# Gain rows of a two-layer decoder put on all partitions by a transpose and by way of memory, instead of by matmuls with diagonals

## The chip, the cores and the metric

The kernel runs on one core of a Trainium2 chip. The metric is the device time of one execution in microseconds (us). PE is TensorE, PEld its weight load, DVE is VectorE, ACT is ScalarE, POOL is GpSimd, SP is SyncE.

## The reference

A decoder of two layers with one sequence of 512 tokens, a model width of 1024, all in fp32. A conditioning vector `c` gives six vectors of 1024 per layer (shift, scale and gain for the mixer, the same for the MLP), by a product with a large matrix. The first layer's mixer is a pooling over windows, the second's a gated unit (SGU).

```python
c_act = jax.nn.silu(c)
for i in range(DEPTH):                                   # 2 layers
    mod = c_act @ ada_w[i] + ada_b[i]                    # 6 x 1024
    sh1, sc1, g1, sh2, sc2, g2 = jnp.split(mod, 6, axis=-1)
    h = modulate(rmsnorm(x, norm_mix_g[i]), sh1, sc1)    # h * (1 + sc) + sh
    y = pool_mixer(h, ...) if i == 0 else sgu_mixer(h, ...)
    x = x + g1[:, None, :] * y
    h = modulate(rmsnorm(x, norm_mlp_g[i]), sh2, sc2)
    x = x + g2[:, None, :] * sq_relu_mlp(h, mlp_w1[i], mlp_w2[i])   # square(relu(h @ w1)) @ w2
return rmsnorm(x, final_g)
```

The change is about `g1` and `g2`: a gain has one value per channel, and the tile `x` has tokens on partitions and channels along a row, so the gain is needed as one row of 1024 that stands alike on all 128 partitions.

## The kernel before, in words

Large products are done as three matmuls each (`mm3`, lines 178 to 180): both operands are split into a high and a low part of a reduced type. ScalarE makes the high part (line 169), VectorE the low part by a subtraction (line 170).

Products of the conditioning vector are done on VectorE: `ada_tile` loads 128 columns of the large matrix (512 KB) into a work buffer of tag `w4` (there are three of these, and raw weights take the same three) and sums them against the vector `cb` (line 200). The results are columns: `mods[i]` has 48 columns of 128 values for layer i, and a gain takes eight of them (`c_g`). The columns become a row on all partitions in `spread_cols`: GpSimd multiplies the identity by each of the eight columns (`diagonals`, line 209), which gives eight 128x128 diagonals in one tile `dg`; two matmuls of a matrix of ones against four diagonals each (line 218, in fp32, not split) put the row on all partitions in PSUM; two ScalarE copies (line 219) bring it into `gb`, one tile of 128x1024 that all gains share in turn. `gated` (line 966) and `fold` (line 837) read it.

There are three spreads. The first, the gain of the first MLP, is an entry of the list `ex` that `mlp` works off beside the matmuls: 33 entries, spread over the units of work by a quota `due`. It stands ninth, behind the eight `ada_tile`s that make its columns. The second, the gain of the SGU, is the first entry of the list in the SGU part, called in `do_u(0)`, after the unit's matmuls. The third, the gain of the second MLP, is in `mlp(1)`, where the diagonals are made ahead (tile `dgu`) and the matmuls come after the unit `("f", (0, 7))`. The first gain of the first layer goes another way that the change doesn't touch.

`mlp(i)` is a list of units: "f" a tile of the up projection, "s" and "p" products of a scheme with seven products in place of eight for the up and the down projection, "q" the rest of the down projection. Operands of a unit are prepared some units ahead (`ahead`, `prep`). In the second layer the weight sums that this scheme needs are partly made by transfers that add to what stands in the buffer, and these are issued by GpSimd:

```python
def b_add(t, c, r, n):
    G.dma_start(t, w2[i, c, r, n], accum_op=ALU.add)      # line 767; line 703 is the like for w1
```

Such a weight tile `bt` (1 MB) is split, added to, split again, added to, and so on. TensorE's instructions run in the order of the code. Those of the other engines and of their DMA queues are ordered at compile time by a scheduler from readiness and the order of the code (by hand in the first layer's mixer). On each engine and each queue of an engine the order is then fixed, and an instruction that waits holds up those behind it. `sm` is a pool of small tiles; the pools are padded (`shift`) so that tiles start at multiples of 128 words.

Of the kernel before, what the change touches and what calls it, by code (L numbers as in the profile page):

```python
# [7 lines left out]
F32 = mybir.dt.float32  # L8
F32R = mybir.dt.float32r
AF = mybir.ActivationFunctionType  # L10
ALU = mybir.AluOpType
# [3 lines left out]
P = 128  # L15
D = 1024
S = 512
KD = D // P
# [23 lines left out]
def c_sh(n, k):  # L42
    return 24 * n + 2 * k + 1


def c_g(n, k):
    return 24 * n + 16 + k
# [31 lines left out]
def decoder_kernel(ctx: ExitStack, tc: tile.TileContext, xtok, vecs, rows, fgrow, ada0, adag, ada1, pool_w, w1s, w1, w1f, w1b, w2, w2e, w_v, w_u, w_o, wsT, lnp, bs, out):  # L79
    nc = tc.nc  # L80
    V, A, G, T = nc.vector, nc.scalar, nc.gpsimd, nc.tensor
# [3 lines left out]
    w4 = ctx.enter_context(tc.tile_pool(name="w4", bufs=3))  # L85
    wts = ctx.enter_context(tc.tile_pool(name="wts", bufs=5))
    cp = ctx.enter_context(tc.tile_pool(name="cp", bufs=1))
    sm = ctx.enter_context(tc.tile_pool(name="sm", bufs=3))
# [17 lines left out]
    def bank(name, pool=None):  # L106
        pool = pool or ps
        return pool.tile([P, S], F32, name=name, tag="mm" if pool is ps else "xz")
# [4 lines left out]
    ones = cp.tile([P, P], F32, name="ones")  # L113
# [3 lines left out]
    ident = cp.tile([P, P], F32, name="ident")  # L117
    G.memset(ident, 0.0)
    G.affine_select(out=ident, in_=ident, compare_op=ALU.not_equal, fill=1.0, base=0, pattern=[[-1, P]], channel_multiplier=1)
    mods = [cp.tile([P, 48], F32, name=f"mods{i}") for i in range(2)]  # L120
# [16 lines left out]
    gb = big.tile([P, D], F32, name="gb")  # L137

    def X(t):
        return x_[t // 2][:, t % 2]  # L140

    def H(k, c):

        return h_[0][:, 0, k, c], h_[0][:, 1, k, c]
# [4 lines left out]
    def mod(i, c):  # L149
        return mods[i][:, c : c + 1]  # L150
# [32 lines left out]
    def finish_mods(i, b, pm):  # L183

        V.tensor_tensor(mods[i][:, 2 * b : 2 * b + 2], pm, vec[:, V_ADAB + 48 * i + 2 * b : V_ADAB + 48 * i + 2 * b + 2], ALU.add)
        n, q = divmod(b, 12)
        if q < 8:
            g0 = (V_MIX, V_MLP)[n] + 8 * i + q
            V.scalar_tensor_tensor(scl[i][n][:, q : q + 1], mod(i, 2 * b), 1.0, vec[:, g0 : g0 + 1], ALU.add, ALU.mult)
# [3 lines left out]
    def ada_tile(i, t, src, get):  # L193

        r = get()
        nc.sync.dma_start(r, src)
        b, j = divmod(t, 2)
        if j == 0:
            pmv[i, b] = sm.tile([P, 2], F32, name="pmv", tag="pmv")
        V.scalar_tensor_tensor(r, r, 1.0, cb, ALU.mult, ALU.mult, accum_out=pmv[i, b][:, j : j + 1])  # L200
        if j == 1:
            finish_mods(i, b, pmv.pop((i, b)))
# [1 line left out]
    def get4():  # L204
        return w4.tile([P, D], F32, name="ada", tag="w4")

    def diagonals(dg, cols):
        for k in range(KD):
            G.tensor_scalar(dg[:, k], ident, cols[:, k : k + 1], None, ALU.mult)

    def spread_cols(cols, dg=None):

        if dg is None:
            dg = w4.tile([P, KD, P], F32, name="dg", tag="w4")
            diagonals(dg, cols)
        for n in range(2):
            po = bank("pb")
            T.matmul(po, ones, dg[:, 4 * n : 4 * n + 4], start=True, stop=True)  # L218
            A.activation(gb[:, S * n : S * n + S], po, AF.Copy)


    def power(v, n):
# [12 lines left out]
    with (  # L235
# [67 lines left out]
        def rms():  # L303
            v0 = sm.tile([P, NT], F32, name="rv4", tag="rv4")
            V.tensor_scalar(v0, ss, RMS_EPS, None, ALU.add)
            rt.append(power(v0, NT))
# [217 lines left out]
        def norm_lo(k):  # L524
# [8 lines left out]
            sm=sums_of, rms=rms, edge=edges, bandr=bands, m=m, n=n_, nf=n_fin, fin=fin, gm=gm, gt=gt, gc=gc, bc=bc, we=we,  # L533
# [58 lines left out]
    def parts(o, a):  # L592

        A.activation(o[0], a, AF.Copy)
        V.tensor_tensor(o[1], a, f32(o[0]), ALU.subtract)

    def mlp(i, first, extra, last, ending):
# [3 lines left out]
        with (  # L601
# [56 lines left out]
            def a_sums(step):  # L658


                def a(r, j):
                    return h32[0][:, 4 * j : 4 * j + 4, 256 * r : 256 * r + 256]

                def operand(pool, tag):
                    t = pool.tile([P, 2, 4, 256], F32R, name="as", tag=tag)
                    return t[:, 0], t[:, 1]

                def minus(o, p, q):
                    V.tensor_tensor(o, p, q, ALU.subtract)

                first, half = slice(0, 256), slice(256, 512)
                if step == 0:
                    sums_a.update({1: H(slice(0, 4), first), 2: H(slice(4, 8), first), 4: H(slice(4, 8), half)})
                    shift(hx, LINE - GAP)
                    minus(a(1, 1), a(1, 0), a(1, 1))
                    m, o = 5, operand(hx, "hx")
                elif step == 1:
                    minus(a(1, 1), a(1, 1), a(0, 0))
                    m, o = 6, operand(big, "x0")
                elif step == 2:  # L680
                    minus(a(0, 0), a(0, 0), a(1, 0))
                    V.tensor_tensor(a(1, 1), a(1, 1), a(0, 1), ALU.add)
                    m, o = 3, operand(big, "x1")
                else:
                    m, o = 7, H(slice(0, 4), half)
                parts(o, a(0, 0) if m == 7 else a(1, 1))
                sums_a[m] = o
# [214 lines left out]

            gain = mods[i][:, c_g(1, 0) : c_g(1, 0) + KD]
            done = first(put)
            if i:
                dg = su.tile([P, KD, P], F32, name="dgu", tag="u")
                diagonals(dg, gain)
            units = [("f", (0, f)) for f in range(done, 8)]
            for c in range(3):
                if i == 0:  # L910
# [17 lines left out]
            def ahead(n):  # L928

                if i == 0:  # L930
                    return min(n + 3, len(units))
                m, s = n + 1, items(*units[n])
                while m < len(units) and m < n + 5:
                    s += items(*units[m])
                    if s > 5 and m > n + 1:
                        break
                    m += 1
                return m
# [4 lines left out]
            for n, (kind, u) in enumerate(units):  # L943
                for m in range(n, ahead(n)):
                    if m not in ready:
                        ready[m] = prep[units[m][0]](units[m][1])
                while at < len(extra) and at < due * (n + 1):
                    extra[at]()
                    at += 1
                run[kind](u, ready[n])  # L950
                if i and kind == "f":
                    a_sums(u[1] - 4)
                    if u == (0, 7):
                        spread_cols(gain, dg)
                if i and u == (3, 1, 4):
                    reload()

# [24 lines left out]
    def normed(hf, i, n):  # L982

        xs = []
        for r in range(2):
            t = w4.tile([P, D], F32, name="xs", tag="w4")
            A.activation(t, X(2 * hf + r), AF.Copy, scale=rms(2 * hf + r))
            xs.append(t)
        c = slice(256 * hf, 256 * hf + 256)
        for k in range(0, KD, 2):  # L990
            px = bank("px")
            for q in range(2):
                for r in range(2):
                    T.transpose(px[:, 256 * q + P * r : 256 * q + P * r + P], xs[r][:, P * (k + q) : P * (k + q) + P], ident)  # L994
            tt = h32[0][:, k : k + 2, c] if h32 else sm.tile([P, 2, 256], F32, name="tt", tag="tmp")
            for q in range(2):
                a, b = scl[i][n][:, k + q : k + q + 1], mod(i, c_sh(n, k + q))
                if q:
                    A.activation(tt[:, q], px[:, 256:512], AF.Identity, bias=b, scale=a)
                else:  # L1000
                    V.tensor_scalar(tt[:, q], px[:, 0:256], a, b, ALU.mult, ALU.add)
            parts(H(slice(k, k + 2), c), tt)


    h32, xd = [], []
    dram = ctx.enter_context(tc.tile_pool(name="dram", bufs=1, space=bass.MemoryType.DRAM))

    def spill(h):
        xd.append(dram.tile([P, 2, D], F32, name=f"xd{h}"))
# [2 lines left out]
    def reload():  # L1012
        for h in range(2):
            x_[h] = big.tile([P, 2, D], F32, name=f"x{h}", tag=f"x{h}")
            G.dma_start(x_[h], xd[h])
        load_fg()
# [4 lines left out]
        return SWEEP  # L1021

    ex = [lambda q=q: ada_tile(0, 40 + q, ada1[q], get4) for q in range(8)]
    ex += [lambda: spread_cols(mods[0][:, c_g(1, 0) : c_g(1, 0) + KD])]
    ex += [lambda q=q: ada_tile(1, q, ada1[8 + q], get4) for q in range(24)]
    mlp(0, first0, ex, gated, lambda: normed(0, 1, 0))


# [6 lines left out]
    with (  # L1035
# [27 lines left out]
        for t in range(NT):  # L1063
# [6 lines left out]
            r = rsqrt(ag[:, 1:2], 1.0, LN_EPS, 1)  # L1070
# [2 lines left out]
                V.tensor_tensor(v, v, lnt[:, n].rearrange("p (a b) -> p a b", a=2), op)  # L1073

        u, gt, wu = {}, {}, {}
        ex = [lambda: spread_cols(mods[1][:, c_g(0, 0) : c_g(0, 0) + KD])]
        ex += [lambda q=q: ada_tile(1, q, ada1[8 + q], get4) for q in range(24, 40)]

        def do_u(n):
# [75 lines left out]
    def last1(t, c0, n, src, y):  # L1155
# [13 lines left out]
        else:  # L1169
# [5 lines left out]
            nc.sync.dma_start(out[t, :, 1], X(t)[:, S:D])  # L1175

    mlp(1, first1, [], last1, lambda: None)


# [77 lines left out]
```

## Time and profile before

| | |
|---|---|
| time, median of 3 runs | 872.88 us (872.5 to 873.39) |
| profiled execution | 872.98 us, its span 871.3 us |
| TensorE busy | 858.0 us, 98% of the span |
| VectorE, ScalarE, GpSimd busy | 669.6, 452.0, 66.2 us |
| granted TensorE clock, mean | 0.998 |
| moved by DMA | 161.80 MB, 186 GB/s |
| GpSimd's DMA queue | 4032 packets, 23.07 MB, 13.0% of the engines' time |

Times in the trace are counted from the start of the span. A row of a group gives line, engine, operation, written and read tiles, shapes and count, then the busy time and the mean length of one in ns, then the engine's idle time just before them and what ended most of it. A row of a timeline gives start, length, the instruction, and in brackets the idle time before it with what ended that. The lengths of matmuls are modelled and overlap; the chain in order of time gives each the stretch until the next one.

### The profile page before, as it was taken

What the parts mean: (1) busy time and instruction counts of PE and PEld (TensorE: products, weight loads), DVE (VectorE), ACT (ScalarE), POOL (GpSimd) and SP (SyncE); (2) the same over time, 40 slices, a digit from 0 to 9 for tenths busy, and PEclk for the clock granted to TensorE, in tenths of its full rate; (3) what the DMA queues carried; (4) which work ended last, traced back from release to release, by engine and by line L of the source; (5) the groups of instructions that cost most, each with busy time, mean ns of one, the idle gap of its engine ahead of it and who ended that gap; (6) DMA issues with size and microseconds to landing.
All of it is one profiled execution on the core that took longest, in us unless ns stands there. A gap on an engine that the chain in (4) does not pass through costs nothing.

```text
span 871.3 us, 11810 instructions
## 1 busy us (share of the span) xinstructions
PE 858.0 (98%) x4580; PEld 739.3 (85%) x4580; DVE 669.6 (77%) x884; ACT 452.0 (52%) x656; POOL 66.2 (8%) x87
## 2 busy tenths in 40 slices
PE   8999999999999999999999999999999999999996
PEld 7778888788888888888878888999999998999885
DVE  6889696789869886657798866667777698778755
ACT  5285755554444445238233326666765576566521
POOL 3000002000000000000410012000101000100001
PEclk9999999999999999999999999999999999999999
DMA  9959853553454341615548525937758587667302
GB/s 352 417 224 316 293 179 129 193 193 121 180 206 169 127 163 49 217 33 209 193 159 291 180 73 210 340 78 179 167 196 181 155 230 220 138 160 261 123 24 97
DMA packets 39517, 161.80 MB, mean 186 GB/s; under 512 B 4387, under 2 KB 4515, under 8 KB 34214
## 3 DMA queue, kind: packets, MB, share of 16 engines
q1 hardware_dynamic: 35282, 137.72, 44.1%
q0 software_dynamic: 4032, 23.07, 13.0%
q8 instruction: 36, 0.59, 0.2%
q10 hardware_dynamic: 148, 0.27, 0.1%
q14 instruction: 19, 0.16, 0.0%
HBM read 156.84 MB, written 4.19 MB: 185 GB/s over the span
## 4 chain that ended last, share of the span: by engine, by line
PE 91%; DMA 5%; DVE 1%; ACT 1%; issue 0%; SPq 0%; POOLq 0%; POOL 0%; DVEq 0%; ACTq 0%
PE po L178 17%; PE po L180 17%; PE po L179 17%; PE pm L178 12%; PE pm L179 12%; PE pm L180 12%; DMA wl<-in_ada 2%; DMA wh<-in_ada 1%; DMA raw<-in_w1s 1%; PE po L1099 1%; ACT sq L275 1%; PE px L994 1%; DMA x<-in_xtok 1%; PE pb L218 1%; PE po L566 0%
## 5 line engine op out<-in xcount | busy, mean ns | idle before, releaser
L178 PE MATMUL po<-hb,wl 128*128 128x256 f32 (+1 forms) x624 | 209.7, 336 | 0.4 <-DVE wl L170 0.4
L180 PE MATMUL po<-hb,wh 128*128 128x256 f32 (+1 forms) x624 | 207.8, 333 | 0.0
L179 PE MATMUL po<-hb,wh 128*128 128x256 f32 (+1 forms) x624 | 207.8, 333 | 0.0
L170 DVE TENSOR_TENSOR wl<-raw,wh 128x1024 fp32r<-128x1024 f32 (+1 forms) x110 | 131.1, 1194 | 47.2 <-ACT wh L169 47.1
L169 ACT ACTIVATE wh<-raw 128x1024 fp32r<-128x1024 f32 (+1 forms) x110 | 113.1, 1034 | 64.8 <-PE pm L180 31.9
L179 PE MATMUL pm<-wl,oh 128*128 128x512 f32 x336 | 130.8, 389 | 0.0
L178 PE MATMUL pm<-wh,ol 128*128 128x512 f32 x336 | 130.8, 389 | 0.0
L180 PE MATMUL pm<-wh,oh 128*128 128x512 f32 x336 | 130.8, 389 | 0.0
L178 PEld LDWEIGHTS po<-hb,wl 128*128 128x128 f32 x624 | 117.2, 188 | 14.1 <-DVE wl L170 1.2
L179 PEld LDWEIGHTS po<-hb,wh 128*128 128x128 f32 x624 | 117.2, 188 | 12.9 <-issue 0.5
L180 PEld LDWEIGHTS po<-hb,wh 128*128 128x128 f32 x624 | 118.0, 189 | 11.9
L170 DVE TENSOR_TENSOR wl<-b,wh 128x1024 fp32r<-128x1024 f32 x60 | 72.9, 1223 | 26.6 <-ACT wh L169 26.5
L200 DVE SCALAR_TENSOR_TENSOR ada<-ada,cb 128x1024 f32<-128x1024 f32 x56 | 68.3, 1222 | 15.4 <-DMA ada<-in_ada 15.3
L180 PEld LDWEIGHTS pm<-wh,oh 128*128 128x128 f32 x336 | 63.1, 188 | 13.1
L179 PEld LDWEIGHTS pm<-wl,oh 128*128 128x128 f32 x336 | 63.1, 188 | 12.2
L178 PEld LDWEIGHTS pm<-wh,ol 128*128 128x128 f32 x336 | 63.1, 188 | 12.3
L169 ACT ACTIVATE wh<-b 128x1024 fp32r<-128x1024 f32 x60 | 63.3, 1056 | 17.4 <-PE pm L180 9.5
L632 ACT ACTIVATE g<-po 128x512 f32<-128x512 f32 x40 | 23.6, 599 | 76.2 <-PE po L180 74.3
L170 DVE TENSOR_TENSOR wl<-bt,wh 128x1024 fp32r<-128x1024 f32 x24 | 29.1, 1224 | 28.0 <-ACT wh L169 28.0
L971 ACT ACTIVATE tmp<-x 128x512 f32<-128x512 f32 (+1 forms) x25 | 15.3, 612 | 64.8 <-DVE x L967 64.7
L859 DVE TENSOR_TENSOR y<-y,pm 128x512 f32<-128x512 f32 x68 | 43.7, 682 | 1.0 <-PE pm L180 1.0
L179 PE MATMUL po<-as,wh 128*128 128x256 f32 x144 | 40.5, 281 | 0.0
(211 smaller groups left out, 1487.6 us busy)
## 6 DMA issues: line engine op xcount, KB each, us to landing
ada<-in_ada SPq DMA_DIRECT2D x72, 512.0 KB, 3.4
b<-in_w SPq DMA_DIRECT2D x21, 1024.0 KB, 5.7
raw<-in_w SPq DMA_DIRECT2D x25, 512.0 KB, 4.0
raw<-in_w1b SPq DMA_DIRECT2D x24, 512.0 KB, 5.7
bt<-in_w POOLq DMA_DIRECT2D x9, 1024.0 KB, 8.0
raw<-in_w2e SPq DMA_DIRECT2D x16, 512.0 KB, 3.2
raw<-in_w1b POOLq DMA_DIRECT2D x12, 512.0 KB, 5.3
wh<-in_ada SPq DMA_DIRECT2D x9, 512.0 KB, 9.6
```

What stands on the lines that cost most here:

```text
L169: A.activation(h[:, c], r[:, c], AF.Copy)
L170: V.tensor_tensor(l[:, c], r[:, c], f32(h[:, c]), ALU.subtract)
L178: T.matmul(o, wl, mh, start=first, stop=False, **kw)
L179: T.matmul(o, wh, ml, start=False, stop=False, **kw)
L180: T.matmul(o, wh, mh, start=False, stop=last, **kw)
L200: V.scalar_tensor_tensor(r, r, 1.0, cb, ALU.mult, ALU.mult, accum_out=pmv[i, b][:, j : j + 1])
L218: T.matmul(po, ones, dg[:, 4 * n : 4 * n + 4], start=True, stop=True)
L275: A.activation(j, X(t)[:, c], AF.Square, scale=D**-0.5, accum_out=out)
L632: A.activation(t, po, AF.Relu)
L859: V.tensor_tensor(yt, yt, banks[hf], ALU.subtract if minus else ALU.add)
L971: A.activation(tmp, xt, AF.Square, scale=D**-0.5, accum_out=s[:, len(cs) : len(cs) + 1])
L994: T.transpose(px[:, 256 * q + P * r : 256 * q + P * r + P], xs[r][:, P * (k + q) : P * (k + q) + P], ident)
```

## The change

`spread_cols` no longer makes diagonals. TensorE transposes the eight columns (128x8) into PSUM (8x128), ScalarE copies that to a small tile `line` (a new tag of the pool `sm`, 128 words on a partition), GpSimd stores it to a tile in memory (4 KB), and then loads it from there into `gb`, the same 1024 values for each of the 128 partitions (512 KB). The diagonals that were made ahead in `mlp(1)` go. The pool for tiles in memory is opened earlier. The first spread moves in its list from the ninth place to the thirteenth.

```diff
-    def diagonals(dg, cols):
-        for k in range(KD):
-            G.tensor_scalar(dg[:, k], ident, cols[:, k : k + 1], None, ALU.mult)
-
-    def spread_cols(cols, dg=None):
-
-        if dg is None:
-            dg = w4.tile([P, KD, P], F32, name="dg", tag="w4")
-            diagonals(dg, cols)
-        for n in range(2):
-            po = bank("pb")
-            T.matmul(po, ones, dg[:, 4 * n : 4 * n + 4], start=True, stop=True)
-            A.activation(gb[:, S * n : S * n + S], po, AF.Copy)
+    dram = ctx.enter_context(tc.tile_pool(name="dram", bufs=1, space=bass.MemoryType.DRAM))
+
+    def spread_cols(cols, name):
+
+        po = bank("pb")[0:KD, 0:P]
+        T.transpose(po, cols, ident)
+        r = sm.tile([KD, P], F32, name="line", tag="line", bufs=1)
+        A.activation(r, po, AF.Copy)
+        line = dram.tile([KD, P], F32, name=name)
+        G.dma_start(line, r)
+        G.dma_start(gb, line.rearrange("(o k) p -> o (k p)", o=1).to_broadcast([P, D]))
@@ mlp
-            if i:
-                dg = su.tile([P, KD, P], F32, name="dgu", tag="u")
-                diagonals(dg, gain)
...
-                        spread_cols(gain, dg)
+                        spread_cols(gain, "gain1")
@@
     ex = [lambda q=q: ada_tile(0, 40 + q, ada1[q], get4) for q in range(8)]
-    ex += [lambda: spread_cols(mods[0][:, c_g(1, 0) : c_g(1, 0) + KD])]
     ex += [lambda q=q: ada_tile(1, q, ada1[8 + q], get4) for q in range(24)]
+    ex.insert(12, lambda: spread_cols(mods[0][:, c_g(1, 0) : c_g(1, 0) + KD], "gain0"))
...
-        ex = [lambda: spread_cols(mods[1][:, c_g(0, 0) : c_g(0, 0) + KD])]
+        ex = [lambda: spread_cols(mods[1][:, c_g(0, 0) : c_g(0, 0) + KD], "gainm")]
```

More of the change, by code (lines that the diff above doesn't have):

```diff
@@ L1005, in decoder_kernel @@
     h32, xd = [], []
-    dram = ctx.enter_context(tc.tile_pool(name="dram", bufs=1, space=bass.MemoryType.DRAM))
     def spill(h):
```

## The prediction

> **What bounds the kernel now.** I read the page first, then the busy time by windows, the chain of work that ended last in order of time, the instructions on the tiles that the change touches, the DMA issues, and last the timeline around the third spread.
>
> ```profile
> span 871.3 us, 11810 instructions
> ...
> PE 858.0 (98%) x4580; PEld 739.3 (85%) x4580; DVE 669.6 (77%) x884; ACT 452.0 (52%) x656; POOL 66.2 (8%) x87
> ...
> PEclk9999999999999999999999999999999999999999
> ...
> PE 91%; DMA 5%; DVE 1%; ACT 1%; issue 0%; SPq 0%; POOLq 0%; POOL 0%; DVEq 0%; ACTq 0%
> ...
> L178 PE MATMUL po<-hb,wl 128*128 128x256 f32 (+1 forms) x624 | 209.7, 336 | 0.4 <-DVE wl L170 0.4
> L180 PE MATMUL po<-hb,wh 128*128 128x256 f32 (+1 forms) x624 | 207.8, 333 | 0.0
> ```
>
> TensorE is busy for 98% of the span at a full granted clock, it makes up 91% of the chain, and in the large groups of matmuls the idle time before them is 0.4 us in all. A stretch taken off TensorE should therefore come off the end, unless another engine turns out to be just behind. The windows show that for the places in question:
>
> ```profile
> 148.00:160.00 12.00, 12.00 (x51) 9.26 (x50) 10.79 (x11) 6.74 (x10) 0.00 (x0) 1.00 0.52 189
> 532.00:544.00 12.00, 11.60 (x74) 9.94 (x73) 11.76 (x23) 9.63 (x19) 3.96 (x5) 1.00 0.69 241
> 580.00:592.00 12.00, 12.00 (x95) 11.04 (x95) 7.37 (x7) 8.65 (x12) 0.85 (x2) 1.00 0.42 70
> ```
>
> The columns after the window's length are the busy times of PE, PEld, DVE, ACT and POOL. Only from 532 to 544 us does TensorE stand still (0.40 us), where VectorE has 11.76 us of work in 12.
>
> **The change part by part. On TensorE.** Each of the three spreads now is two fp32 matmuls of the ones against eight diagonals, and becomes one transpose of a 128x8 block. Both kinds stand in the chain, in order of time (start, length, what):
>
> ```profile
> 158.39 1.72 PE pb L218 x4
> ...
> 388.63 1.75 PE px L994 x16
> ...
> 446.58 1.72 PE pb L218 x4
> ...
> 585.44 1.72 PE pb L218 x4
> ```
>
> A spread holds TensorE 1.72 us (two matmuls, four records). The 16 transposes of 128x128 at line 994 hold it 1.75 us, 1.75/16 = 0.11 us each. The new transpose streams the 128 columns of the identity in the same way against only eight loaded columns, so 0.11 us is my value. From above I bound it by one record of line 218, 1.72/4 = 0.43 us, in case a lone small instruction pays for the change of kind at its edges; from below there is nothing cheaper in these rows. Saved: 1.72 - 0.11 = 1.61 us a spread, 3 x 1.61 = **4.83 us**; with 0.43 it is 3.87 us.
>
> **On ScalarE and GpSimd**, off the path:
>
> ```profile
> L219 ACT ACTIVATE gb<-pb x6: 579/588/598, 159.4 to 587.9; 128x512 f32<-128x512 f32 x6
> ...
> L209 POOL TENSOR_SCALAR dg<-ident,mods x16: 597/602/2672, 137.6 to 420.0; 128x128 f32<-128x128 f32 x16
> ...
> L281 ACT ACTIVATE ca<-vec 128x8 f32<-128x8 f32 x1 | 0.2, 208 | 0.0
> ```
>
> ScalarE loses two copies of 0.59 us per spread and gains one of 8x128. Between the 0.21 us of the 128x8 row and 0.59 us I take 0.3, so it has 0.9 us less to do. GpSimd loses eight products per spread. A work buffer (the three of tag w4) is no longer held by the diagonals in the first two spreads. All this can only help an engine for which TensorE waits 0.4 us in all, so it is worth between 0 and 0.4 us; I take 0.
>
> **The new wait.** The row goes 128x8 to 8x128 to memory (4 KB), and from there to all partitions (512 KB). GpSimd issues both, and before the second it has to wait until the first has landed. Queued behind that wait is whatever else GpSimd does. As to the row itself, these are its readers and what is near:
>
> ```profile
> L966 DVE TENSOR_TENSOR tmp<-y,gb x15: 689/692/694, 356.8 to 859.0; 128x512 f32<-128x512 f32 x15
> L966 DVE TENSOR_TENSOR tmp<-po,gb x8: 684/691/692, 503.2 to 539.4; 128x512 f32<-128x512 f32 x8
> ...
> L837 DVE TENSOR_TENSOR y<-y,gb x1: 686/686/686, 806.1 to 806.1; 128x512 f32<-128x512 f32 x1
> ```
>
> The first gain row is read from 356.8 us on, the second from 503.2 to 539.4, the third from 806.1. The spreads stand at 158, 447 and 585, so each has more than 55 us until a reader comes (the first almost 200, less what it moves), and no old reader is still open. The first one also moves: from ninth in the list of extra work to thirteenth, which at 33 entries over 48 units is six units later. Its last column is there long before:
>
> ```profile
> 137.44 0.16 DVE L185 TENSOR_TENSOR mods<-pmv,vec 128x2 f32<-128x2 f32 x1
> ...
> 444.86 2.42 POOL L225 TENSOR_TENSOR rr<-rv,mhalf 128x1 f32<-128x1 f32 x2 [8.77 <-DVE rv L230]
> ...
> 448.05 4.63 DVE L1073 TENSOR_TENSOR v<-v,lnt 128x1024 f32<-128x1024 f32 x4
> ...
> 464.66 0.89 PE po L1099 x8
> ```
>
> At the second spread GpSimd still has two reciprocal roots of the layer norm, over at 447.3. If they came behind the new wait, the norm (done at 452.7) would move by that wait, and the matmuls that read it begin at 464.66: 12 us of cover.
>
> **The third spread is the tight place.** There GpSimd also issues the additions that VectorE leaves to the DMA (line 767, weights of the second layer's down projection):
>
> ```profile
> 588.57 0.84 POOL L767 DMA_DIRECT2D bt<-in_w  x1 [8.57 <-DVE wl L170]
> 601.01 0.85 POOL L767 DMA_DIRECT2D bt<-in_w  x1 [11.59 <-DVE wl L170]
> ...
> 587.44 1.07 ACT L219 ACTIVATE gb<-pb 128x512 f32<-128x512 f32 x2
> ...
> 609.11 1.06 ACT L169 ACTIVATE wh<-bt 128x1024 fp32r<-128x1024 f32 x1 [2.13 <-DMA bt<-in_w]
> ...
> 610.20 1.23 DVE L170 TENSOR_TENSOR wl<-bt,wh 128x1024 fp32r<-128x1024 f32 x1 [1.69 <-ACT wh L169]
> ...
> 617.66 0.39 PE L178 MATMUL pm<-wh,ol 128*128 128x512 f32 x1
> ```
>
> ```profile
> out<-x SPq DMA_DIRECT2D x7, 256.0 KB, 2.0
> ada<-in_ada SPq DMA_DIRECT2D x72, 512.0 KB, 3.4
> xd<-x POOLq DMA_DIRECT2D x2, 1024.0 KB, 6.7
> ...
> DMA to landing us min/median/max: 7.7/8.1/10.8
> ```
>
> The last row is that of line 767. In the times of this trace: the small copy stands where the two gb copies stand, so the row is ready at 587.44 + 0.3 = 587.74. The first transfer lands d later, issuing the second takes 0.85 (the length of an issue at 767), and GpSimd is free at 588.59 + d, where it would have issued the addition at 588.57. The addition is late by X = d, or by nearly nothing if it is put ahead of the second transfer. For d no row has 4 KB from GpSimd. The stores of 256 KB land in 2.0 us; with half a microsecond for GpSimd's slower issue (0.84 in the rows of 767) I take 2.5. The far end is 10.8, the longest landing at line 767. The additions form a series: the first, at 588.57, delays the second, at 601.01, for which ScalarE waits at 609.11. Its first half is split at 610.20 + 1.23 = 611.43 and wanted at 617.66: 6.2 us of room. TensorE is 1.6 us earlier after this spread and the addition's trigger is not, so 4.6 us are left. X = 2.5 is hidden; beyond 4.6 every microsecond is one on TensorE.
>
> The Trainium skill's page "DMA: Bandwidth & Descriptors" has a fit for GpSimd's transfers, in "Anatomy of one DMA — SWDGE (gpsimd) path": 2.0 us plus bytes over 436e3. By it, as an estimate, d would be 2.0 us, hidden as well, and the sum would not change.
>
> **Does the saving pass 532 to 544?** VectorE's full stretch starts on TensorE's signal, after idle time:
>
> ```profile
> 531.76 0.69 DVE L966 TENSOR_TENSOR tmp<-po,gb 128x512 f32<-128x512 f32 x1 [2.97 <-PE po L180]
> ```
>
> So it begins earlier when TensorE is earlier, and the two earlier savings pass.
>
> **The sum.** The profiled execution took 872.98 us (span 871.3 and 1.68 around it), 0.1 above the median of 872.88. 872.98 - 4.83 = 868.15, so **868.2 us**. With 0.43 us per transpose it is 869.1; with the 0.4 us of stall gone too it is 867.7. The runs before spread 0.4 us below and 0.5 above their median, so this case alone reaches from 867.2 to 869.1.
>
> **The rivals.** *The second transfer in front of the addition.* If both go through GpSimd's queue in order of issue, the addition also waits for 512 KB, 3.4 us by the loads of ada: X = 2.5 + 3.4 = 5.9, 1.3 us over the room: 869.5 us. For it: both leave from one queue on the page. Against it: the second transfer need not be issued first, and transfers overlap. The same page of the Trainium skill, in "SWDGE vs HWDGE vs iDMA", says that of the queues for GpSimd's transfers only one is allocated, which speaks for this rival; no row here shows two of them waiting on one another.
>
> *The wait on GpSimd holds up TensorE: slower.* It takes the third spread alone. With d = 10.8 and 3.4 of the second transfer, X = 14.2, 9.6 us of stall at 617.66 (before), 872.98 - 4.83 + 9.6 = 877.8 us. It ends slower than before from X = 4.6 + 4.8 = 9.4 us on. For it: the spill's 6.7 us shows that writes to memory from GpSimd can be long. Against it: that is 1 MB, the row is 4 KB, and the DMA share around 585 us is 0.42.
>
> *The first two savings are given back* at 532 to 544, if VectorE is held there by something that doesn't follow TensorE, such as a load: only the third remains, 872.98 - 1.61 = 871.4 us. Against it: the 2.97 us of idle time released by PE.
>
> **How the numbers follow.** Forecast 0.72, transfer in front 0.10, savings given back 0.08, slower 0.10. A measurement of this kernel tells about 0.2% (1.7 us) from no change: below 871.1 is faster, which takes the first two, 0.82; given back is the same, 0.08; slower is 0.10. The range goes from 867.2 over the second case and most of what lies short of the third, to 871.0; left out are the last two, 0.18.
>
> **What would show it.** Right: three groups of one 128-column transpose in place of four records of 0.43 us, PE's busy time down by about 4.8 us, still no idle time before lines 178 to 180, and GpSimd's second issue 2 to 3 us after its first. Wrong: a wait of PE for wl at the second down product after the third spread (released by bt), or ScalarE waiting for bt much longer than 2.1 us there; PE's busy time down but the span not, with new idle time near 532; transposes that take over 0.4 us; or matmuls of a changed length anywhere.

## The result, and the profile after

The change makes the kernel faster by about 3 us: 869.75 us, median of 8 runs (868.48 to 871.9), against 872.83 for the kernel before beside it, a ratio of 0.9964 (0.995 to 0.9978). Two repetitions of the same kernel gave 0.9969 (0.9957 to 0.998) and 0.9974 (0.9961 to 0.9988). The forecast was 868.2 us in a range of 867.2 to 871.0. The time lies inside it, but 1.5 us over the forecast, near the 869.5 us of the rival "the second transfer in front of the addition". The execution profiled took 871.33 us with a span of 869.3; it is at the slow end of the runs, and part of this section is about why.

The page, and the tile `pb` with its row `line` (name, count, shortest, median and longest length in ns, first and last start):

```profile
span 869.3 us, 11768 instructions
...
PE 855.5 (98%) x4571; PEld 738.5 (85%) x4571; DVE 668.0 (77%) x884; ACT 448.4 (52%) x653; POOL 49.4 (6%) x69
...
L178 PE MATMUL po<-hb,wl 128*128 128x256 f32 (+1 forms) x624 | 209.1, 335 | 0.9 <-DVE wl L170 0.9
...
L178 PE MATMUL po<-as,wl 128*128 128x256 f32 x144 | 40.5, 281 | 0.5 <-DVE wl L170 0.5
```

```profile
L212 PE MATMUL pb<-ident,mods x3: 271/271/272, 190.7 to 584.4; 128*8 128x128 f32 x3
L214 ACT ACTIVATE line<-pb x3: 248/250/252, 191.4 to 585.1; 8x128 f32<-8x128 f32 x3
```

Nine records have gone from TensorE (4580 to 4571: twelve fp32 records out, three transposes in), but its busy time fell only by 2.5 us, and there is new idle time of 0.5 us in front of each of two groups: 0.9 us where 0.4 stood for `po<-hb,wl`, and 0.5 for `po<-as,wl`. The 0.27 us of a transpose isn't what it holds; the timeline of TensorE at the first spread tells that by the starts:

```profile
190.52 0.39 PE L180 MATMUL po<-hb,wh 128*128 128x512 f32 x1
190.75 0.27 PE L212 MATMUL pb<-ident,mods 128*8 128x128 f32 x1
190.77 0.47 PE L178 MATMUL po<-hb,wl 128*128 128x512 f32 x1
191.09 0.39 PE L179 MATMUL po<-hb,wh 128*128 128x512 f32 x1
```

Two 512-column matmuls stand 0.23 us apart here. From 190.52 to 191.09 there are two such steps, 0.46 us, and 0.11 us more: that is the transpose. By the starts of the same matmuls in both profiles, TensorE gains 1.64, 1.61 and 1.61 us at the three spreads, 4.86 in all.

At the end it is 2.00 us ahead. The rest goes where the two profiles differ in other places. TensorE stands 0.72 + 0.24 us at 546 and 551, and with the steps beside these waits its lead falls by 0.83 + 0.36. It stands 0.68 us at 623, where the lead falls by 0.81. A slower pace of its matmuls from 547 to 584 costs 1.35, and 0.29 of that comes back right after the third spread, where the kernel before is the slower one. It was 0.12 us ahead before the first spread, and the kernel before loses 0.10 more at 541: 4.86 + 0.12 + 0.10 - 0.83 - 0.36 - 0.81 - 1.35 + 0.29 = 2.02.

The wait at 623 is downstream of the third spread. GpSimd there (timeline: start, length, instruction, idle time before it):

```profile
585.61 0.57 POOL L216 DMA_DIRECT2D gain<-line  x1 [8.22 <-ACT line L214]
587.55 0.57 POOL L217 DMA_DIRECT2D gb<-gain  x1 [1.38 <-DMA gain<-line]
588.53 0.89 POOL L765 DMA_DIRECT2D bt<-in_w  x1 [0.41 <-DVE wl L170]
602.87 0.86 POOL L765 DMA_DIRECT2D bt<-in_w  x1 [13.45 <-DVE wl L170]
```

The first addition (line 765 now, 767 before) is issued at 588.53, in the kernel before at 588.57: GpSimd's new wait of 1.38 us was over by then and didn't delay it. It still waited 0.41 us for VectorE's subtraction. That subtraction comes late, though. TensorE was 0.9 us ahead at this place and the subtraction was not, because the compiled order has changed: ScalarE now makes `line` and `g` ahead of the split of `bt`, and VectorE makes the sum `s` ahead of the subtraction; in the kernel before, the copies into `gb`, `g` and the sum stood behind. The split and the subtraction, first in the kernel before, then in the changed one:

```profile
585.97 1.05 ACT L169 ACTIVATE wh<-bt 128x1024 fp32r<-128x1024 f32 x1
587.05 1.23 DVE L170 TENSOR_TENSOR wl<-bt,wh 128x1024 fp32r<-128x1024 f32 x1 [0.62 <-ACT wh L169]
...
585.74 1.04 ACT L169 ACTIVATE wh<-bt 128x1024 fp32r<-128x1024 f32 x1
587.01 1.22 DVE L170 TENSOR_TENSOR wl<-bt,wh 128x1024 fp32r<-128x1024 f32 x1
```

And the addition landed later. The landings of line 765 (shortest, median, longest; the first addition is the longest):

```profile
DMA to landing us min/median/max: 7.8/8.2/10.6
```

It had taken 7.9 us before. The next addition can be issued only when VectorE is done with this one's result, at 602.87 where 601.01 stood, and it takes 9.06 us to land where 8.02 stood. What ScalarE did with it, and the chain of waits in order of time:

```profile
612.02 1.06 ACT L169 ACTIVATE wh<-bt 128x1024 fp32r<-128x1024 f32 x1 [4.64 <-DMA bt<-in_w]
```

```profile
602.87 9.06 DMA bt<-in_w
...
612.02 1.06 ACT wh L169
...
614.26 0.95 ACT wh L169
615.21 0.97 ACT y L860 x2
616.18 0.95 ACT wh L169
...
618.30 1.22 DVE ol L593
...
621.35 1.06 ACT wh L169
...
622.44 1.24 DVE wl L170
...
623.81 0.36 PE po L178
```

```profile
623.01 0.28 PE L180 MATMUL po<-hb,wh 128*128 128x256 f32 x1
623.81 0.36 PE L178 MATMUL po<-as,wl 128*128 128x256 f32 x1 [0.52 <-DVE wl L170]
```

ScalarE stands 4.64 us for `bt` (2.13 before) and begins the split at 612.02 (609.11 before). Behind that instruction are other splits and copies in its fixed order, behind them VectorE's, and at the end of the row the weights of an up product, `po<-as`, that have nothing to do with the addition. TensorE's next start comes 0.80 us after the last instead of 0.12.

The earlier wait has to do with another load, the fourth raw tile of the up projection (ScalarE's timeline):

```profile
544.80 1.06 ACT L169 ACTIVATE wh<-raw 128x1024 fp32r<-128x1024 f32 x1 [2.84 <-DMA raw<-in_w1f]
```

ScalarE waits 2.84 us for it; the kernel before waited 1.02.

### The profile page after: what moved, and what is told of

It reads as the page before. It is cut to its first block, busy times and chain, and to the rows that moved or that the text cites. A ratio compares the mean times of both kernels' runs of the same rounds, so it can differ in the third digit from the quotient of the medians.

```text
span 869.3 us, 11768 instructions
## 1 busy us (share of the span) xinstructions
PE 855.5 (98%) x4571; PEld 738.5 (85%) x4571; DVE 668.0 (77%) x884; ACT 448.4 (52%) x653; POOL 49.4 (6%) x69
## 5 line engine op out<-in xcount | busy, mean ns | idle before, releaser
L178 PE MATMUL po<-as,wl 128*128 128x256 f32 x144 | 40.5, 281 | 0.5 <-DVE wl L170 0.5
```

The lines of the kernel that those rows point to most:

```text
L178: T.matmul(o, wl, mh, start=first, stop=False, **kw)
```

## The experiments

Four questions were asked: is the wait at 623 that of the transfers, and by which of them; is the wait at 546 due to the change; what sets the pace; and what would a version without the costs take. All line numbers below are those of the kernel named.

**The same kernel again.**

> The changed kernel once more, beside the next three. Theory: of the 4.7 us that TensorE saves, about 1 us is given back at a wait near 546 us and 1.3 us by slower 256-column matmuls behind it (117.8 instead of 113.3 ns), and 0.7 us at 623 us. These waits hang on when a load lands, so the time varies from run to run between about 868.5 and 872 us, median 869 to 870.5. Rival (the slower matmuls come with the new placement of tiles): 117.8 ns from 547 to 584 us in every profile, wait or no wait.

870.56 us (869.57 to 871.49, 6 runs), 0.9969 (0.9957 to 0.998). Its profile has no wait at 546 or 551 and the quick pace from 547 to 582, but again a wait at 621 (0.89 us; it is the one at 623, earlier because TensorE is), and a new one near 777 (0.65). So the first two are not fixed properties of the new order; the one at 621 is there again.

**The third spread later**, behind the first four down products:

```diff
-                    if u == (0, 7):
-                        spread_cols(gain, "gain1")
+                if i and (kind, u) == ("p", (0, 3)):
+                    spread_cols(gain, "gain1")
```

> The third spread comes after the down product (0, 3), some 50 us later, when no addition of weights is due on GpSimd. Theory (the 512 KB of the row go in front of the first addition on the way out): the first addition lands about 8 us after its issue (10.6 us in the changed kernel), and the wait of 0.7 us at 623 us is gone; the time is 0.4 us less or so. Rival (the wait at 623 us is of ScalarE and VectorE being full, the row has no part in it): the wait stays.

869.3 us (868.0 to 871.45, 6), 0.9961 (0.9946 to 0.9976). The first addition, now issued ahead of the transfers, lands after 8.5 us, and the wait at 621 is gone from the trace. The intervals of this and the repetition overlap, so the gain can't be told by the time alone.

**The fourth raw tile in a buffer of its own**, to let its load start earlier:

```diff
         wf = [split(raw4(w1f[f]), 1 if f else 4) for f in range(n)]
# becomes, for the last f:
+            r = su.tile([P, D], F32, name="raw", tag="u")
+            nc.sync.dma_start(r, w1f[f])
```

> The raw weights of the fourth tile of the second layer's first products get a buffer of their own (the place of the former diagonals), so that their load needn't wait for one of the three work buffers. Theory: the wait of 0.72 us at 546 us goes, the 256-column matmuls behind it run at 113.3 ns up to 584 us, and the time is about 2 us less than the changed kernel's (867 to 868.5) and varies less. Rival one (placement sets the pace): the wait goes, but the pace stays at 117.8 ns and only 0.7 us is won. Rival two (the load is slow for the traffic around it, not for the buffer): wait and time stay.

874.89 us (873.61 to 876.57, 9), 1.002 (1.001 to 1.003): slower, as no theory had it. The work buffer that came free was filled by the next load, and the scheduler put the split of that load ahead of the norm on ScalarE. ScalarE's timeline, then the windows (length; busy time of PE, PEld, DVE, ACT, POOL with instructions; granted clock, DMA share, GB/s):

```profile
548.62 1.06 ACT L169 ACTIVATE wh<-raw 128x1024 fp32r<-128x1024 f32 x1 [5.57 <-DMA raw<-in_w1f]
549.58 1.00 ACT L994 ACTIVATE h<-px,mods,scl 128x256 f32<-128x256 f32 x2
```

```profile
550.00:553.00 3.00, 1.51 (x8) 1.31 (x9) 2.22 (x3) 3.00 (x8) 0.93 (x1) 0.92 1.01 378
553.00:557.00 4.00, 4.00 (x24) 4.00 (x24) 2.76 (x4) 1.90 (x4) 0.00 (x0) 0.63 0.98 205
557.00:560.00 3.00, 3.00 (x29) 3.00 (x28) 2.97 (x3) 2.54 (x5) 0.00 (x0) 1.00 0.85 175
```

TensorE waits 2.6 us in two pieces, and then the granted clock averages 0.63 over 4 us. The run says nothing on the wait at 546, but it shows again what one waiting split does to the instructions behind it.

**More small transposes**, 19 copies of the 128x8 one in other places, to see whether they set the pace:

```diff
+                if (i, u) == (1, (0, 4)):
+                    T.transpose(po[0:KD, 0:P], gain, ident)
...
+                    T.transpose(banks[0][0:KD, 0:P], gain, ident)
```

> As the changed kernel, with one transpose of 128x8 more (into a bank that the next product overwrites) ahead of the up product (0, 4) and ahead of each of the 18 up products of the second layer that open a bank. Theory (the pace is a rhythm between weight loads and matmuls into which TensorE falls; a small transpose starts the quick one, a wait or a run of 512-column matmuls the slow one): 113.3 ns from there on until the next 512-column product; 1.2 us less from 550 to 584 us, and in the other 18 places 0.1 us of extra transpose against 0.11 to 0.3 us won, so 1 to 3 us less in all. Rival (the pace goes with the operands' places or with the traffic): 117.8 ns stays, and the 19 transposes cost 2 us.

872.34 us (870.1 to 873.15, 11), 0.9984 (0.9975 to 0.9993). That is 1.8 us over the repetition. That a small transpose starts the quick pace was wrong. A lone one switches between the two paces, in either direction: from 113 to 118 ns at 559.8 and 621.9, from 118 to 113 at 585.6, 607.7 and 619.1; two in a row left it as it was, and one at 645.4 did too.

**The third spread as before**, the first two new:

```diff
-                        spread_cols(gain, "gain1")
+                        spread_old(dg)      # diagonals ahead, two fp32 matmuls, two copies
```

> The third spread by diagonals and matmuls as before, the first two by way of memory. Theory: the first two save 1.6 us each and nothing is given back at 623 us, as no row goes in front of the additions there; the wait near 546 us is there in some executions and not in others. About 869.5 to 871.5 us, near the changed kernel, because the third spread's 1.6 us and the 0.7 to 1.0 us that it costs at 623 us nearly cancel. Rival (the wait at 623 us comes from TensorE being ahead, not from the row): a wait at 623 us also here.

870.36 us (869.74 to 872.27, 8), 0.9972 (0.9962 to 0.9983). The addition lands after 8.3 us and nothing waits at 621. This is as fast as the whole change within the interval: the third spread earns 1.6 us on TensorE, and the wait near 621 takes 0.6 to 0.9 of that back.

**Both transfers of all three spreads issued by SyncE:**

```diff
-        G.dma_start(line, r)
-        G.dma_start(gb, line.rearrange(...)...)
+        nc.sync.dma_start(line, r)
+        nc.sync.dma_start(gb, line.rearrange(...)...)
```

> All three spreads' transfers issued by SyncE instead of GpSimd. Theory: the row no longer goes in front of the first addition, which lands some 8 to 9 us after its issue, and the wait at 623 us is gone; but SyncE stands still while the 4 KB land, and they queue behind weight loads of the same queue, so weight loads behind it come 2 to 6 us later, three times. Where these are loaded several units ahead that costs nothing: 868.5 to 870 us. Rival (the loads behind it are wanted at once): new waits of 1 us or more near 190, 446 or 585 us, and a time above the changed kernel's.

868.04 us (867.49 to 869.26, 5), 0.9948 (0.9935 to 0.9961), the lowest ratio of all the kernels here. SyncE's queue and TensorE at the place of the wait:

```profile
583.07 0.29 SPq L216 DMA_DIRECT2D gain<-line  x1
584.29 0.33 SPq L217 DMA_DIRECT2D gb<-gain  x1
```

```profile
621.04 0.28 PE L180 MATMUL po<-hb,wh 128*128 128x256 f32 x1
621.16 0.28 PE L178 MATMUL po<-as,wl 128*128 128x256 f32 x1
```

The addition lands after 8.4 us, and the next matmul comes 0.12 us after the last. TensorE is 3.18 us ahead of the kernel before in front of the third spread, 4.79 behind it and 4.77 at its last matmul: what this spread saves arrives whole. Issued by SyncE, the same 512 KB no longer hold up the addition. That need not be due to the other queue: SyncE gets from the store to the load in 1.2 us (1.9 on GpSimd), and the load is issued 2.0 us ahead of the addition (issued at 586.25) instead of 1.0. By the DMA packets in the trace the load moved from 585.3 to 587.4 and the addition's first packet began at 587.8, so the two never met. In the changed kernel the load moved from 588.8 to 593.2 and the addition's first packet began at 590.4. No run parts the other queue from the earlier start.

**The third load cut to 64 of its 1024 columns:**

```diff
+        n = D if name != "gain1" else 64
-        G.dma_start(gb, line.rearrange(...).to_broadcast([P, D]))
+        G.dma_start(gb[:, 0:n], line.rearrange(...)[:, 0:n].to_broadcast([P, n]))
```

> The third spread loads only the first 64 of the 1024 columns of its row (32 KB instead of 512 KB; the rest of the row is left out and stays the second gain). Store, wait and issue on GpSimd stay. Theory (the 512 KB in front delay the addition): it lands after 8 to 8.5 us instead of 10.6 to 11, and the wait of 0.7 to 1.0 us at 621 to 623 us goes. Rival (the wait on GpSimd between the two transfers delays it): the addition is issued as late as before and the wait at 623 us stays.

869.82 us (869.36 to 870.44, 6), 0.9963 (0.9952 to 0.9975). GpSimd's timeline, and TensorE's:

```profile
586.07 0.58 POOL L218 DMA_DIRECT2D gb<-gain  x1 [1.38 <-DMA gain<-line]
587.05 0.89 POOL L766 DMA_DIRECT2D bt<-in_w  x1 [0.40 <-DVE wl L170]
599.36 0.86 POOL L766 DMA_DIRECT2D bt<-in_w  x1 [11.42 <-DVE wl L170]
```

```profile
621.84 0.28 PE L180 MATMUL po<-hb,wh 128*128 128x256 f32 x1
621.95 0.28 PE L178 MATMUL po<-as,wl 128*128 128x256 f32 x1
```

GpSimd waits as long as with the full load (1.38 us, then 0.40), and ScalarE and VectorE have the same order of instructions as in the changed kernel, but the addition lands after 8.5 us and TensorE doesn't wait at 621. It is the 512 KB, not the wait on GpSimd. ScalarE's own wait for `bt` is no sign of it: it is 5.2 us here, longer than the 4.64, and 5.1 with all by SyncE; what counts is when it ends.

**The third row loaded twice**, the first time into a tile that is no longer read:

```diff
+        for to in (cb, gb) if name == "gain1" else (gb,):
+            G.dma_start(to, line.rearrange(...).to_broadcast([P, D]))
```

> The third spread loads its row twice, first to a tile that nobody reads any more, then to its place: 1 MB in front of the first addition. Theory: the addition lands some 13 us after its issue, and the wait at 621 to 623 us grows by about the 2.5 us that the transfer adds, to some 3.5 us; the time is 2.5 us above the changed kernel's. Rival (the row goes beside the addition, and its lateness has another cause): landing and wait as in the changed kernel, the time within 0.5 us of it.

871.39 us (870.21 to 873.5, 10), 0.9981 (0.997 to 0.9992). GpSimd's timeline, the landings of its line 766, and TensorE:

```profile
585.13 0.57 POOL L218 DMA_DIRECT2D cb<-gain  x1 [1.38 <-DMA gain<-line]
585.69 0.53 POOL L218 DMA_DIRECT2D gb<-gain  x1
586.21 0.93 POOL L766 DMA_DIRECT2D bt<-in_w  x1
```

```profile
DMA to landing us min/median/max: 7.9/8.6/12.9
```

```profile
622.12 0.28 PE L180 MATMUL po<-hb,wh 128*128 128x256 f32 x1
623.45 0.36 PE L178 MATMUL po<-as,wl 128*128 128x256 f32 x1 [1.04 <-DVE wl L170]
```

With 32 KB in front the addition takes 8.5 us, with 512 KB 10.2 to 11.0 (three profiles of the changed kernel), with 1 MB 12.9. TensorE's waits in 612 to 624 are 0, 0.57 to 0.89, and 1.03 + 1.21 us, less than the 3.5 expected. So this wait needs the load in front of the addition, and grows with it.

**The change once more, the third spread alone by SyncE, and all three by SyncE once more**, side by side:

```diff
-        G.dma_start(line, r)
+        q = nc.sync if name == "gain1" else G
+        q.dma_start(line, r)      # and the load likewise
```

> The changed kernel beside the two with SyncE, on the same chip. 869.5 to 870.7 us; a wait of 0.7 to 1 us at 621 to 623 us.

> Only the third spread's transfers by SyncE, the first two by GpSimd. Theory (what GpSimd's queue costs is the third spread alone): no wait at 621 to 623 us, and the time is as with all by SyncE, 868 to 869 us. Rival (the first two cost something as well): the time lies between that of all by SyncE and the changed kernel's.

> All three by SyncE once more: 867.5 to 869 us, 1 to 2 us under the changed kernel, with no wait after 552 us; a wait of less than 1 us near 546 us may come in some executions.

They gave 870.9 us (869.17 to 875.36, 12 runs), 870.37 (868.72 to 872.36, 7) and 869.14 (867.76 to 871.48, 6): ratios of 0.9974 (0.9961 to 0.9988), 0.9962 (0.9948 to 0.9977) and 0.9953 (0.9937 to 0.997). The medians fall from the first to the last, but the intervals overlap. In the traces the wait at 621 is 0.57 us in the first and 0 in the other two. The waits elsewhere come with and without it, as the table shows; with them the second kernel missed its 868 to 869 us, and the third has a wait near 777 that wasn't expected.

**The kernel before once more**, for those other waits:

> The kernel before once more, for a second profile of it. Theory (the wait near 546 us in the changed kernel comes of a load that lands between 4.6 and 7.5 us after its issue, with the same lead in both kernels, and isn't of the change): the load of the fourth tile's raw weights may land late here too, and where it takes over 6 us TensorE waits near 550 us. Likewise an addition that takes over 9 us brings a wait near 781 us. Rival (both come only with the change): the load lands within 5.2 us and the addition within 8.3, and there is no wait at either place.

873.26 us (872.44 to 873.88, 8), 0.9995 (0.9983 to 1.0006) to itself. It has no such wait, and the slower pace. The raw tile took 4.9 us, as the rival had it. An addition issued at 759.73 took 9.35 us, and there was no wait behind it, against the theory.

All profiles side by side. The waits are TensorE's, in us, by the starts of its matmuls; "landed" is the time from issue to landing of the first addition after the third spread, and "raw tile" the time from the issue of the fourth raw tile's load to ScalarE's use (with the fourth tile in its own buffer: of the load behind it).

| kernel | raw tile | wait 546 to 551 | landed | wait near 621 | wait near 777 | span |
|---|---|---|---|---|---|---|
| before | 5.0 | 0 | 7.9 | 0 | 0 | 871.3 |
| before again | 4.9 | 0 | 8.0 | 0 | 0 | 872.1 |
| after | 6.8 | 0.96 | 10.6 | 0.68 | 0 | 869.3 |
| after again | 4.65 | 0 | 11.0 | 0.89 | 0.65 | 868.3 |
| after, third time | 7.9 | 2.18 | 10.2 | 0.57 | 0 | 869.0 |
| third spread later | 7.0 | 1.12 | 8.5 | 0 | 0 | 866.7 |
| fourth tile's own buffer | 8.2 | 2.61 | 10.4 | 0.98 | 0.77 | 872.5 |
| more transposes | 5.5 | 0 | 10.9 | 0.99 | 0.43 | 869.8 |
| third as before | 5.2 | 0 | 8.3 | 0 | 0.27 | 869.1 |
| small load | 6.3 | 0.59 | 8.5 | 0 | 0.37 | 867.7 |
| row loaded twice | 5.8 | 0.16 | 12.9 | 2.24 | 0.49 | 869.5 |
| third by SyncE | 7.3 | 1.55 | 8.4 | 0 | 1.05 | 869.0 |
| all by SyncE | 5.5 | 0 | 8.4 | 0 | 0 | 866.3 |
| all by SyncE again | 6.5 | 0.75 | 8.4 | 0 | 0.47 | 867.1 |

The column "near 621" follows "landed": 8.5 us and less give no wait, 10.2 and more always one. The column "546 to 551" follows the raw tile's load: 5.5 us and less give no wait, 5.8 and more always one. Why that load takes longer in most changed kernels is open. Its lead over its use is the same (8.4 us from issue to TensorE's need, before and after), it shares the DMA engines with 1 MB of spill and 2 MB of other weights, and two profiles of before against twelve of changed kernels don't tell whether the change does it. Where the third spread goes by diagonals (before, before again, third as before) it takes 4.9 to 5.2 us, elsewhere 4.65 to 8.2; that is a hint and no more.

The wait near 777 has the same form as the one near 621. The chain of "third by SyncE" has it behind an addition, with splits and a subtraction between:

```profile
756.16 10.33 DMA bt<-in_w
...
778.78 0.36 PE po L178
```

In the profiles with this wait, the two additions issued near 743 and 756 land after 18.6 to 19.4 us together, in those without it after 16.5 to 17.9. No spread's transfer is near. Why these additions land later is open, and so is whether the change does it: the wait appears only in changed kernels, but not in all of them.

## Why the prediction was right or wrong

**TensorE's term was right.** It said 1.61 us a spread; 1.61 to 1.64 were measured, and the transpose holds 0.11 to 0.12 us, the value taken from sixteen larger ones. The bound of 0.43 wasn't needed.

**The side terms were right.** The small copy takes 0.25 us (0.3 said). The first two spreads are covered as argued, and the saving passes 532 to 544: TensorE is 3.3 to 3.4 us ahead at 541.

**The size of d was near:** the 4 KB landed 1.7 us after their issue in the median and 2.3 to 2.7 at most (three profiles), where 2.5 was taken. The Trainium skill's fit ("DMA: Bandwidth & Descriptors", "Anatomy of one DMA — SWDGE (gpsimd) path") gave 2.0 us, and the rows agree with it to 0.7.

**The step that failed is "X = 2.5 is hidden".** It went wrong in three places. First, the delay is not where it was looked for. X was to be the lateness of the addition's issue through GpSimd's wait, with the small copy where the two copies into `gb` had stood. The copy came earlier, GpSimd's wait was over before the addition was due, and the second transfer was issued in front of it. The delay is in the transfer: 7.9 us became 10.6. That was the rival given 0.10, and its mechanism is what the runs showed, though with a different price: 2.2 to 3.1 us for 512 KB (10.2 to 11.0, less 7.9 to 8.0), nothing from d, and 0.57 to 0.89 us on TensorE where 1.3 was said. The Trainium skill's rule behind that rival, that of the queues for GpSimd's transfers only one is allocated ("DMA: Bandwidth & Descriptors", "SWDGE vs HWDGE vs iDMA"), agrees with the packets: the load's and the addition's are all of one queue, `q0` on the page. The objection "transfers overlap" was half true. The addition's packets begin beside the load's, but at 593.0, 4.45 us after its issue, 18 of 128 have begun where 62 had in the kernel before, and some of these take up to 3.0 us where none took over 1.6.

Second, the trigger of the addition was taken as unchanged but for TensorE's lead. By the new order on ScalarE and VectorE it comes 0.9 us later against TensorE, in the kernels with SyncE too.

Third, the room of 4.6 us (6.2 less the third spread's own 1.6) was counted to one reader, the second down product at 617.66. That product was in time: the split of `bt` is 612.02 - 609.11 = 2.91 us later and TensorE 2.80 us earlier, which is 5.71 of the 6.2. The wait came a product later, through instructions that stand behind the waiting split on ScalarE and VectorE. For them 5.0 us are covered: in three profiles of the changed kernel the two terms sum to 5.71, 5.91 and 5.59 us, and the waits are 0.68, 0.89 and 0.57; with the small load or SyncE the sum is 3.7 to 4.0. The 2.91 us are not the load's alone: 1.86 are the later issue of the second addition, and 1.04 its own landing (9.06 us against 8.02). This second landing takes 8.6 to 9.9 us in every kernel whose third spread goes by way of memory at this place, by SyncE too, and 8.0 to 8.5 in the other four profiles; why is open.

**Not priced at all** were the raw tile's load (0 to 2.2 us in three profiles of the same kernel), the pace (1.35 us from 547 to 584 in one of them), and the wait near 777 (0 to 0.65). The kernel before had none of these waits in two profiles, so there was no row to price them from. In three profiles of the changed kernel the waits sum to 1.64, 1.54 and 2.75 us; 4.86 less these is 2.1 to 3.3, against 2.4 to 3.1 by the medians. Of that, only the wait near 621 is shown to come of the change. That the time came out near the 869.5 us of the rival is therefore in part luck: the rival's wait was about half its price, and terms that nobody had priced made up the rest. **The rivals that failed:** the first two savings weren't given back at 532 to 544, and GpSimd's wait of 1.38 us was hidden.

**What a better version is:** with the transfers on SyncE's queue the time was 868.04 and 869.14 us, 0.9948 and 0.9953 of the kernel before; the first of these is what the prediction's sum had without any cost.

## What to carry to other kernels

When a transfer is added to a queue, price it for what is queued behind it in that queue: a load nobody waits for delayed the next transfer of GpSimd by 2 to 3 us and cost TensorE 0.6 to 0.9. Issuing it from SyncE, which also issued it a microsecond earlier, removed that cost. And count the room of a delayed operand not only to its own reader: the instruction that waits for it holds up everything behind it on its engine, and a product that doesn't use the operand may be the first to be late. Last, read the order on each engine again after a change: here other instructions came to stand ahead of the one that mattered, for 0.9 us.

## What the runs showed of the hardware

Back-to-back matmuls of 256 columns run at one of two steady paces, 113.3 or 117.8 ns from start to start, at the same granted clock. Windows of before, of before again, of after and of after again, in this order (the PE count tells them apart):

```profile
560.00:572.00 12.00, 12.00 (x108) 12.00 (x107) 9.23 (x9) 8.45 (x13) 0.00 (x0) 1.00 0.62 209
```

```profile
560.00:572.00 12.00, 12.00 (x104) 12.00 (x104) 10.30 (x10) 9.52 (x14) 0.66 (x1) 1.00 0.63 209
```

```profile
560.00:572.00 12.00, 12.00 (x104) 12.00 (x103) 10.37 (x10) 7.68 (x11) 0.86 (x1) 1.00 0.46 149
```

```profile
560.00:572.00 12.00, 12.00 (x108) 12.00 (x108) 10.12 (x10) 7.98 (x11) 0.86 (x1) 1.00 0.48 151
```

Both kernels have both paces, so it isn't the change that sets it; over 34 us it makes 1.3 us. A single small instruction between them often switches it, and directly after a group of 512-column matmuls it was always 117.8 in the second layer's MLP. What decides was not found.

The clock fell after a short wait. Where the split was put ahead of the norm, TensorE waited 2.0 and 0.6 us within 549 to 552, and from 553 to 557 only 24 matmuls ran, where 35 fit at 113 ns; at first their starts stood 213 ns apart. Waits of 1.78 and 0.39 us at the same place (after, third time) didn't lower the granted clock. The Trainium skill ("TensorE: Matmul & The Clock Gate", "Part 1: The HAM clock gate (the "warmup" mystery)") has a state at half the clock after an idle window of about 3.4 us; 213 ns for 256 columns agrees with that state, and the wait here was shorter than its window.
